# The first products of a hybrid decoder's feed-forward and spatial gate by tokens, 256 or 512 columns wide

## The chip, the core and the metric

The kernel runs on one core of a Trainium2 chip: TensorE (matmuls), VectorE, ScalarE, GpSimd, SyncE (which here only issues transfers) and 16 DMA engines. The metric is the time of one execution on the device in microseconds; the kernel before took 1311.81 us (median of three runs, 1311.23 to 1313.46). In the rows and the code the engines are PE, DVE, ACT, POOL and SP.

## The reference

Two layers, each of three sub-layers with a LayerNorm behind them, on x of 256 tokens by 1024 features in float32:

```python
x = LN(ALPHA*x + 0.5*swiglu(x, ffn_w1[l,0], ffn_w3[l,0], ffn_w2[l,0]))   # D_FF = 2816
y, v_raw = hybrid_mixer(x, w_in[l], gate_b[l], p_branch[l], w_out[l], ...)
x = LN(ALPHA*x + y)
x = LN(ALPHA*x + 0.5*swiglu(x, ffn_w1[l,1], ffn_w3[l,1], ffn_w2[l,1]))

swiglu(x, w1, w3, w2) = (silu(x @ w1) * (x @ w3)) @ w2
hybrid_mixer: z = x @ w_in, cut in r k v w a g | zu zv | lx ly | three gates
  o_rwkv = rwkv7(z[r..g])            # state recurrence, 8 heads of 64
  o_gmlp = gelu(zu) * (tril(ws) @ LN(gelu(zv)) + sb)      # spatial gate, 512 wide
  o_lru  = gelu(ly) * scan(conv(lx))                      # 512 wide
  merged = sum(sigmoid(gate_i) * (o_i @ p_branch[i]));  y = merged @ w_out
```

## The kernel before

**Products.** float32 products are made of two parts of each operand: hi is the value rounded to TensorE's fp32r, lo the rest. `mm3` makes each product of a k block (128 of the 1024 inputs) as three matmuls into one accumulator: hi·hi (L214), hi·lo (L215) and lo·hi (L216). x is held transposed as `xT`, hi and lo, 128 features by 256 tokens for each of eight k. There are two forms of product with x. By features (`feature_wide`, the rows w L328 and L330), a weight block is the stationary side and xT the moving one, 512 columns for hi and lo together. By tokens (`token_major`), xT's 128 tokens of a token tile `tt` (two of them) are the stationary side and the weights the moving one: there the output has tokens on its partitions. Before, a block by tokens is 256 columns wide, so that it takes 8 k × 3 = 24 matmuls a token tile.

**What goes by tokens.** In each of the four FFNs block 0 of w1 and of w3 (the rows w1t, w3t), in each mixer the spatial gate's zv (blocks 9 and 10) and zu (blocks 7 and 8), each as two blocks of 256 columns beside each other in one PSUM bank. All other blocks of the FFN (`up(j)`, j from 1 to 10) go by features. `gate` makes silu(h1)·h3 of block 0, `gtrans` transposes it on TensorE to feature-major (gtr), and `split` cuts that in hi and lo (L219, L220). `down(j)` multiplies g by w2 into four accumulators (the rows dn), 2 tt × 2 halves × 2 k × 3 = 24 matmuls of 512 columns a block.

**Weights.** The class `Weights` holds one queue of pieces in the order of use. A piece is 512 KB; SyncE issues its DMA, ScalarE casts it to hi (whi L104), VectorE subtracts for lo (wlo L106; GpSimd does it for the first block of the second FFN of a layer, POOLW). `use(key)` asks for the next piece, and keeps 4 pieces converted ahead of the one in use; with the three or five loads ahead of that, this is what spreads the transfers and conversions over the program.

**The seams.** Each sub-layer ends in a LayerNorm per token tile and in transposes of its result to the next xT (`x_transposes`, the rows tr, two quarters of four transposes for each token tile). `behind(flush, products, cuts)` places a list of products around the two quarters of token tile 1: all but the last cuts[0] before the first quarter, cuts[0] − cuts[1] between, and cuts[1] after the second. FLUSH gives the cuts in groups of three matmuls, (3, 2): the products of token tile 0 that need only its own half of xT fill the time until the transposes of token tile 1 can run. At the start of the program there is nothing to flush: x comes transposed from memory, and `warm` fills in transposes of the identity (L1407). `FHOLD` is 3: the last three blocks of down products are held back to the end of the FFN.

**The mixer.** Its sub-tasks are interleaved by a table (TUNE) and by priorities; a scheduler that simulates the engines then fixes the order of each engine's instructions, which each engine runs strictly in that order. Part of it is one inverse per layer, for the rwkv recurrence. TensorE makes scores sc (L856), transposes bk and ar·v (bkt L866, avt L872); ScalarE copies them; VectorE masks sc, reduces and scales (vs L878, sv L879), and makes X from sc by transposes (L896) and UT from X (L899, L900). GpSimd then runs 30 short steps, X L918 and UT L919 by turns. VectorE makes X L931, Rd L934 and Tt L935 of the result, and TensorE takes that up with y L941, then z, and a second y L959. In the meantime TensorE works off products of the other branches: lx, zu, gate, sg (the spatial mix), ogt (transposes of the spatial gate's result, L1167), lg (the LRU's small products) and ly.

## Time and profile before

| | us |
|---|---|
| median of three runs (lowest to highest) | 1311.81 (1311.23 to 1313.46) |
| the profiled execution, its own time | 1312.26 |
| its span | 1310.5 |
| TensorE busy (9520 matmuls) | 1285.9 (98%) |
| its weight loads, which overlap the matmuls | 1160.5 (89%) |
| VectorE busy | 939.9 (72%) |
| ScalarE busy | 652.6 (50%) |
| GpSimd busy | 84.1 (6%) |
| DMA, mean over the span | 176 GB/s |

The profile is one execution. Its page gives each engine's busy time, the chain of work that ended last, and the costliest groups of instructions; the trace behind it gives every instruction with its start. Matmuls are pipelined, so the duration of one (0.28 us for 256 columns, 0.39 us for 512) is longer than the distance from its start to the next start. The time of a row of them is therefore read from starts. A wait in a row is the engine's idle time before the instruction, with the instruction on another engine that released it. The granted clock is the share of TensorE's 2.4 GHz that the chip let it have.

### The profile page before, as it was taken

Reading aid. Unit: us, or ns where it says so; the run is one execution under the profiler, and the core shown is the slowest. Engines: PE = TensorE matmul, PEld = TensorE weight load, DVE = VectorE, ACT = ScalarE, POOL = GpSimd, SP = SyncE. Lnnn points to the kernel's source line nnn. Section 1 sums busy time; section 2 is a strip of 40 time slices with the busy share of each in tenths; the row PEclk is TensorE's granted clock in tenths of the full one; section 3 lists DMA queues with packets and bytes.
Section 4 is the critical chain, followed back from the end, with each engine's and each line's share of the span. In section 5 each row is a group of like instructions: output and inputs, shape, how many; then the busy total and the mean of one; then the engine's idle time right before and its main releaser. Section 6 shows DMA issues by size and latency. Waiting matters only on the chain.

```text
span 1310.5 us, 23332 instructions
## 1 busy us (share of the span) xinstructions
PE 1285.9 (98%) x9520; PEld 1160.5 (89%) x9520; DVE 939.9 (72%) x1311; ACT 652.6 (50%) x881; POOL 84.1 (6%) x147
## 2 busy tenths in 40 slices
PE   9999999998999999999999999999989999999997
PEld 8888889997999988888898888999979998888886
DVE  6877666787576678666678766667876667787664
ACT  5654426655845545444255544275557544554440
POOL 1000000003000110000000000001030002100000
PEclk9999999999999999999999999999989999999999
DMA  7885524533345658655259664254332466586630
GB/s 264 296 334 192 176 81 130 177 119 125 98 130 177 209 175 311 220 188 171 93 204 355 210 189 140 66 186 129 130 98 99 129 213 206 177 307 214 189 110 33
DMA packets 66843, 230.87 MB, mean 176 GB/s; under 512 B 8208, under 2 KB 8208, under 8 KB 66736
## 3 DMA queue, kind: packets, MB, share of 16 engines
q1 hardware_dynamic: 66096, 227.29, 51.9%
q0 software_dynamic: 640, 2.10, 0.5%
q8 instruction: 75, 1.23, 0.4%
q14 instruction: 32, 0.26, 0.1%
HBM read 228.30 MB, written 1.05 MB: 175 GB/s over the span
## 4 chain that ended last, share of the span: by engine, by line
PE 92%; DVE 4%; POOL 2%; ACT 1%; issue 1%; DVEq 0%; ACTq 0%; POOLq 0%
PE w L328 22%; PE w L330 11%; PE dn L216 6%; PE dn L215 6%; PE dn L214 6%; PE gate L215 3%; PE gate L216 3%; PE gate L214 3%; PE zr L216 2%; PE zr L215 2%; PE zr L214 2%; PE pb L214 2%; PE pb L216 2%; PE pb L215 2%; DVE wlo L106 1%
## 5 line engine op out<-in xcount | busy, mean ns | idle before, releaser
L106 DVE TENSOR_TENSOR wlo<-raw,whi 128x1024 fp32r<-128x1024 f32 (+1 forms) x314 | 379.0, 1211 | 167.7 <-ACT whi L104 97.0
L104 ACT CAST whi<-raw 128x1024 fp32r<-128x1024 f32 (+1 forms) x322 | 327.8, 1034 | 297.3 <-issue 65.6
L328 PE MATMUL w<-xT,whi 128*128 128x512 f32 x1280 | 320.8, 392 | 0.0
L328 PEld LDWEIGHTS w<-xT,whi 128*128 128x128 f32 x1280 | 232.2, 189 | 43.9
L330 PEld LDWEIGHTS w<-xT,wlo 128*128 128x128 f32 x1280 | 174.6, 190 | 12.5
L330 PE MATMUL w<-xT,wlo 128*128 128x256 f32 x1280 | 178.4, 282 | 0.0
L216 PE MATMUL dn<-w,g 128*128 128x512 f32 x352 | 137.5, 390 | 1.5 <-DVE g L220 1.5
L215 PE MATMUL dn<-w,g 128*128 128x512 f32 x352 | 137.2, 390 | 0.0
L214 PE MATMUL dn<-w,g 128*128 128x512 f32 x352 | 137.2, 390 | 0.0
L106 DVE TENSOR_TENSOR w<-raw,w 128x1024 fp32r<-128x1024 f32 x88 | 105.1, 1221 | 37.0 <-ACT w L104 36.9
L401 DVE TENSOR_REDUCE h<-w 128x256 f32<-128x512 f32 x160 | 109.7, 686 | 12.6 <-PE w L330 11.8
L104 ACT CAST w<-raw 128x1024 fp32r<-128x1024 f32 x88 | 89.4, 1048 | 47.5 <-DMA raw<-in_ffn_w_dram 26.0
L214 PE MATMUL gate<-xT,whi 128*128 128x256 f32 x384 | 109.8, 286 | 0.5 <-DVE xc L1187 0.5
L216 PE MATMUL gate<-xT,wlo 128*128 128x256 f32 x384 | 109.7, 286 | 0.0
L215 PE MATMUL gate<-xT,whi 128*128 128x256 f32 x384 | 109.4, 285 | 0.0
L216 PEld LDWEIGHTS dn<-w,g 128*128 128x128 f32 x352 | 66.1, 188 | 15.6 <-DVE g L220 1.9
L214 PEld LDWEIGHTS dn<-w,g 128*128 128x128 f32 x352 | 66.2, 188 | 12.4
L215 PEld LDWEIGHTS dn<-w,g 128*128 128x128 f32 x352 | 66.1, 188 | 12.4
L214 PEld LDWEIGHTS gate<-xT,whi 128*128 128x128 f32 x384 | 73.5, 191 | 1.7 <-issue 1.5
L216 PEld LDWEIGHTS gate<-xT,wlo 128*128 128x128 f32 x384 | 73.5, 191 | 0.6 <-issue 0.2
L215 PEld LDWEIGHTS gate<-xT,whi 128*128 128x128 f32 x384 | 73.5, 191 | 0.5 <-issue 0.2
L219 ACT CAST g<-gf 128x512 fp32r<-128x512 f32 (+1 forms) x44 | 25.6, 581 | 95.0 <-DVE gf L384 95.0
(335 smaller groups left out, 2247.4 us busy)
## 6 DMA issues: line engine op xcount, KB each, us to landing
raw<-in_ffn_w_dram SPq DMA_DIRECT2D x263, 512.0 KB, 4.4
raw<-in_w_in_dram SPq DMA_DIRECT2D x108, 512.0 KB, 3.9
raw<-in_p_branch_dram SPq DMA_DIRECT2D x24, 512.0 KB, 3.5
raw<-in_w_out_dram SPq DMA_DIRECT2D x16, 512.0 KB, 4.2
ln_g<-in_ln_g_dram SPq DMA_DIRECT2D x8, 256.0 KB, 6.1
ln_b<-in_ln_b_dram SPq DMA_DIRECT2D x8, 256.0 KB, 6.5
bd<-in_bd_dram SPq DMA_DIRECT2D x6, 256.0 KB, 6.2
xt<-in_xt_dram SPq DMA_DIRECT2D x4, 256.0 KB, 4.9
```

The source lines that it names most:

```text
L104: self.last_act = self.nc.scalar.copy(hi[:, s:s + w], t[:, s:s + w]).ins
L106: eng.tensor_tensor(lo[:, s:s + w], t[:, s:s + w], hi[:, s:s + w], ALU.subtract)
L214: mm(out, a[0], b[0], start=start, stop=False)
L215: mm(out, a[0], b[1], start=False, stop=False)
L216: self.last_mm = mm(out, a[1], b[0], start=False, stop=stop).ins
L219: self.split_ins = (self.nc.scalar.copy(hi, src).ins, self.nc.vector.tensor_tensor(lo, src, hi, ALU.subtract).ins)
L328: mm(out, parts[0][k], self.xT2[:, :, k, :], start=k == 0, stop=False)
L330: mm(out[:, 0, :], parts[1][k], self.xT[0][:, k, :], start=False, stop=k == 7)
L401: nc.vector.tensor_reduce(t[:, m, :], b.rearrange("p a s -> p s a"), mybir.AxisListType.X, ALU.add)
```

## The change

Block 0 of w1 and of w3 are laid beside each other in memory as one block of 512 columns, w13, and so are zv's two blocks and zu's two. They come as four pieces of [128, 2, 512], each with two k for all 512 columns, in place of 2 × 2 pieces of [128, 4, 256] with four k for 256 columns; number and bytes of the pieces stay as they were. A product by tokens of them is now one matmul of 512 columns where there were two of 256: 48 in place of 96 for each FFN, zv and zu. The FFN takes one PSUM bank per token tile (w13t) in place of two.

`behind` now gets single matmuls, with FLUSH (5, 3): 19 of 512 columns stand before the first quarter of transposes, 2 between, 3 after. Before it was 39 of 256 columns, 3 and 6. In the first FFN of the program, w13's products go k pair by k pair over both token tiles, the filler after the first six; and the first down products of that FFN are used and queued one block later (after up(3), before after up(2)).

```diff
@@ -40,13 +40,13 @@
 FHOLD = 3
 
 
-POOLW = ("w1", "w3")
+POOLW = True
 
 
 HPX = 200
 
 
-FLUSH = (3, 2)
+FLUSH = (5, 3)
 FTAIL = (2, 2)
 
 
@@ -304,11 +304,17 @@
             for f in products[n - cuts[1]:]:
                 f()
 
-    def token_major(self, out, ws, tt, c0, ks=range(8)):
+    def token_major(self, out, ws, tt, ks=range(8)):
 
         for k in ks:
-            self.mm3(out[:, c0:c0 + 256], [t[:, k, tt * P:(tt + 1) * P] for t in self.xT],
-                     [t[:, k % 4, :] for t in ws[k // 4]], k == 0, k == 7)
+            self.mm3(out, [t[:, k, tt * P:(tt + 1) * P] for t in self.xT], [t[:, k % 2, :] for t in ws[k // 2]], k == 0, k == 7)
+
+    def token_products(self, out, ws, tt):
+
+        def product(k, i, j):
+            self.last_mm = self.nc.tensor.matmul(out, self.xT[i][:, k, tt * P:(tt + 1) * P], ws[k // 2][j][:, k % 2, :],
+                                                 start=k + i + j == 0, stop=k == 7 and i == 1).ins
+        return [lambda a=(k, i, j): product(*a) for k in range(8) for i, j in ((0, 0), (0, 1), (1, 0))]
 
     def feature_major(self, out, ws):
 
@@ -333,11 +339,18 @@
         for q in range(2):
             self.W.add(key + (q,), w[c0 // 256, q], pool=pool)
 
+    def queue_wide(self, key, w, pool=False):
+
+        for q in range(4):
+            self.W.add(key + (q,), w[q], pool=pool)
+
+    def use_wide(self, *key):
+        return [self.W.use(key + (q,)) for q in range(4)]
+
     def use_block(self, *key):
         return [self.W.use(key + (q,)) for q in range(2)]
 
 
-    NTM = 1
     HOLD = FHOLD
 
     def queue_ffn(self, l, f):
@@ -349,14 +362,13 @@
-        for w, nm in ((w1, 'w1'), (w3, 'w3')):
-            for j in range(self.NTM):
-                self.queue_block((l, f, nm, j), w, j * 256, pool=f == 1 and nm in POOLW)
+
+        self.queue_wide((l, f, 'w13'), A['w13'][l, f], f == 1 and POOLW)
         d = 0
-        for j in range(self.NTM, NFF):
+        for j in range(1, NFF):
             self.queue_block((l, f, 'w1', j), w1, j * 256)
             self.queue_block((l, f, 'w3', j), w3, j * 256)
-            if j > self.NTM and d < NFF - self.HOLD:
+            if j > 1 + (l + f == 0) and d < NFF - self.HOLD:
                 down(d)
                 d += 1
         while d < NFF:
@@ -366,7 +378,7 @@
     def ffn(self, l, f, x, flush, out=None, between=None):
 
 
-        nc, W, NTM, HOLD = self.nc, self.W, self.NTM, self.HOLD
+        nc, W, HOLD = self.nc, self.W, self.HOLD
         with ExitStack() as ctx:
             tp = ctx.enter_context(self.tc.tile_pool(name=self.n("ffn"), bufs=2))
             xT = self.xT
@@ -419,60 +431,45 @@
             def use_down(j):
                 return [W.use((l, f, 'w2', j, k)) for k in range(2)]
 
-            first = [(nm, [self.use_block(l, f, nm, j) for j in range(NTM)]) for nm in ('w1', 'w3')]
-            gfs, hs = [], {}
+            first = self.use_wide(l, f, 'w13')
+            hs = [self.bank(self.mm, [P, 512], "w13t") for tt in range(2)]
             if flush is None:
 
-                steps = {'w1': ((0, 0, 2), (0, 2, 4), (1, 0, 4), (0, 4, 8), (1, 4, 8)), 'w3': ((0, 0, 8), (1, 0, 8))}
                 last = None
-                for nm, blocks in first:
+                for k in range(0, 8, 2):
                     for tt in range(2):
-                        hs[tt, nm] = self.bank(self.mm, [P, NTM * 256], nm + "t")
-                    for n, (tt, k0, k1) in enumerate(steps[nm]):
                         with ExitStack() as order:
                             if last is not None:
                                 order.enter_context(self.tc.issue_after(last))
-                            self.token_major(hs[tt, nm], blocks[0], tt, 0, range(k0, k1))
+                            self.token_major(hs[tt], first, tt, range(k, k + 2))
                         last = self.last_mm
-                        if nm == 'w1' and n == 0:
+                        if k + tt == 0:
                             with self.tc.issue_after(last):
                                 last = self.warm(WARM[1])
-            for tt in range(2):
-                ps = []
-                for nm, blocks in first:
-                    if flush is None:
-                        ps.append(hs[tt, nm])
-                        continue
-                    b = self.bank(self.mm, [P, NTM * 256], nm + "t")
-                    ps.append(b)
-                    for j in range(NTM):
-                        if tt == 0 and (nm, j) == ('w3', NTM - 1):
-                            self.behind(flush, [lambda k=k: self.token_major(b, blocks[j], tt, j * 256, [k]) for k in range(8)], FLUSH)
-                        else:
-                            self.token_major(b, blocks[j], tt, j * 256)
-                gfs.append(gate(*ps))
-            for j in range(NTM):
-                gtile(j)
+            else:
+                self.behind(flush, self.token_products(hs[0], first, 0), FLUSH)
+                self.token_major(hs[1], first, 1)
+            gfs = [gate(h[:, 0:256], h[:, 256:512]) for h in hs]
+            gtile(0)
 
             def gtrans(tt):
-                ps = self.bank(self.acc, [P, 2 * NTM, P], "gtr")
-                for i in range(2 * NTM):
+                ps = self.bank(self.acc, [P, 2, P], "gtr")
+                for i in range(2):
                     nc.tensor.transpose(ps[:, i, :], gfs[tt][:, i * P:(i + 1) * P], self.ident)
-                for j in range(NTM):
-                    self.split(*[t[:, :, tt * P:(tt + 1) * P] for t in g[j]], ps[:, 2 * j:2 * j + 2, :])
+                self.split(*[t[:, :, tt * P:(tt + 1) * P] for t in g[0]], ps)
 
             d = 0
-            for j in range(NTM, NFF):
+            for j in range(1, NFF):
                 up(j)
...
-                if j == NTM:
+                if j == 1:
                     gtrans(0)
                     gtrans(1)
-                if j > NTM and d < NFF - HOLD:
+                if j > 1 + (l + f == 0) and d < NFF - HOLD:
                     ws = use_down(d)
                     down(d, ws, 0)
                     down(d, ws, 1)
@@ -590,12 +587,12 @@
         def p(b, j):
             T.W.add((l, 'p', b, j), pb[b, j])
 
-        z(9, 10)
+        T.queue_wide((l, 'zv'), A['w_tok'][l, 1])
         for what, *i in beside(l):
             if what == "z":
                 z(ZBLOCKS[i[0]])
             elif what == "zu" and i[0] == 0:
-                z(7, 8)
+                T.queue_wide((l, 'zu'), A['w_tok'][l, 0])
             elif what == "lx":
                 z(11 + i[0])
             elif what == "ly":
@@ -1106,25 +1103,17 @@
         nc.scalar.activation(q, q, AF.Tanh)
         nc.vector.scalar_tensor_tensor(out, q, 1.0, ps, ALU.add, ALU.mult)
 
-    def token_block(self, blocks, tt, what):
-
-        ps = self.mm([P, 512], what)
-        for i, ws in enumerate(blocks):
-            self.T.token_major(ps, ws, tt, i * 256)
-            yield ps
-
     def zv_first(self):
-        T, nc = self.T, self.nc
-        blocks = [T.use_block(self.l, 'z', b) for b in (9, 10)]
+        T = self.T
+        ws = T.use_wide(self.l, 'zv')
         self.gv = []
         for tt in range(2):
             g = self.mt([P, 512], "gv")
             ps = self.mm([P, 512], "zv")
-            T.token_major(ps, blocks[0], tt, 0)
             if tt == 0:
-                T.behind(self.flush, [lambda k=k: T.token_major(ps, blocks[1], tt, 256, [k]) for k in range(8)], FLUSH)
+                T.behind(self.flush, T.token_products(ps, ws, tt), FLUSH)
             else:
-                T.token_major(ps, blocks[1], tt, 256)
+                T.token_major(ps, ws, tt)
             self.gelu2(ps, g)
             self.gv.append(g)
 
@@ -1133,11 +1122,13 @@
         v = nc.vector
         og = [self.mp.tile([P, 2, S], F32R, tag="m", name=T.n("ogT")) for i in range(4)]
         self.og = [[og[0], og[1]], [og[2], og[3]]]
-        blocks = [T.use_block(self.l, 'z', b) for b in (7, 8)]
+        ws = T.use_wide(self.l, 'zu')
         us = []
         for tt in range(2):
             u = self.mt([P, 512], "u")
-            for pu in self.token_block(blocks, tt, "zu"):
+            pu = self.mm([P, 512], "zu")
+            for k in (0, 4):
+                T.token_major(pu, ws, tt, range(k, k + 4))
                 yield self.ZUS
             self.gelu2(pu, u)
             us.append(u)
@@ -1482,8 +1473,16 @@
     r = {n: a[n] for n in big}
 
     r['xt'] = a['x'].reshape(2, P, 2, 4, P).transpose(0, 2, 4, 3, 1)
+    def by_tokens(w):
+        w = w.reshape(w.shape[:-2] + (4, 2, P, 512))
+        i = w.ndim - 4
+        return w.transpose(tuple(range(i)) + (i, i + 2, i + 1, i + 3))
+
     for n in ('ffn_w1', 'ffn_w3', 'w_in'):
         r[n] = pieces(a[n])
+
+    r['w13'] = by_tokens(np.concatenate([a['ffn_w1'][..., 0:256], a['ffn_w3'][..., 0:256]], -1))
+    r['w_tok'] = np.stack([by_tokens(a['w_in'][..., c * 256:(c + 2) * 256]) for c in (7, 9)], 1)
     r['p_branch'] = pieces(a['p_branch'])[:, :, :, 0]
     r.update(vecs=vecs, wsm=wsm, bd=bd)
     return {n: np.ascontiguousarray(t) for n, t in r.items()}
```

The order in three places, each as the instructions stand on their engine.

TensorE in layer 1, where the 19 products of zu that stand behind the last sc end and the transposes of the inverse begin; zu is the spatial gate's product, bkt and avt are the inverse's transposes. Before, then after:

```order
L214 MATMUL zu_10152<-whi_9945,xT_8750 128x256
L866 MATMUL bkt_9879<-ident,bk_9670 128x128 x4
L215 MATMUL zu_10152<-wlo_9946,xT_8750 128x256
L216 MATMUL zu_10152<-whi_9945,xT_8750 128x256
L872 MATMUL avt_9886<-ident,arv_9669 128x128 x4
```

```order
L214 MATMUL zu_9850<-whi_9731,xT_8496 128x512
L863 MATMUL bkt_9577<-ident,bk_9368 128x128 x4
L869 MATMUL avt_9584<-ident,arv_9367 128x128 x2
L863 MATMUL bkt_9593<-ident,bk_9368 128x128 x4
L869 MATMUL avt_9600<-ident,arv_9367 128x128 x2
L869 MATMUL avt_9584<-ident,arv_9367 128x128
```

The products of zu are as many and twice as wide; the first avt, whose four transposes came in one piece behind one bkt, is now parted around the second bkt.

VectorE in layer 1, from the work beside GpSimd's steps to the transposes that y takes up (wlo is a weight piece's subtraction, X L931 or L928 reads GpSimd's last step, u belongs to the spatial gate, xc to the LRU). Before, then after:

```order
L106 TENSOR_TENSOR wlo_10142<-raw_10127,whi_10141 128x1024
L1187 SCALAR_TENSOR_TENSOR xc_10023<-lx_10024,vecs_7883,xc_10023 128x253
L931 TENSOR_SCALAR X_9915<-UT_9920,bsel 128x16x16 x2
L106 TENSOR_TENSOR wlo_10148<-raw_10133,whi_10147 128x1024
L934 STREAM_TRANSPOSE Rd_10283<-X_9915 128x16x2x16
L1160 SCALAR_TENSOR_TENSOR u_10151<-sg_10302,vecs_7883,u_10151 128x128 x4
L106 TENSOR_TENSOR wlo_10392<-raw_10139,whi_10391 128x1024
L935 STREAM_TRANSPOSE Tt_10284<-Rd_10283 128x512
```

```order
L106 TENSOR_TENSOR wlo_9840<-raw_9825,whi_9839 128x1024
L1178 SCALAR_TENSOR_TENSOR xc_9721<-lx_9722,vecs_7629,xc_9721 128x254
L106 TENSOR_TENSOR wlo_9846<-raw_9831,whi_9845 128x1024
L1178 SCALAR_TENSOR_TENSOR xc_9721<-lx_9722,vecs_7629,xc_9721 128x253
L928 TENSOR_SCALAR X_9613<-UT_9618,bsel 128x16x16 x2
L1151 SCALAR_TENSOR_TENSOR u_9849<-sg_9952,vecs_7629,u_9849 128x128 x4
L106 TENSOR_TENSOR wlo_10042<-raw_9837,whi_10041 128x1024
L931 STREAM_TRANSPOSE Rd_9933<-X_9613 128x16x2x16
L932 STREAM_TRANSPOSE Tt_9934<-Rd_9933 128x512
```

One wlo has moved from behind X L931 to ahead of it, among the work beside GpSimd.

TensorE in layer 0, ahead of the second group of scores. Before (34 products of lx stand there, then 14 more of lx and 9 of gate behind the scores), then after (all 48 of lx and 12 of gate ahead, 17 of gate behind):

```order
L216 MATMUL lx_3131<-xT_1897,wlo_2780 128x256
L214 MATMUL lx_3131<-xT_1897,whi_2779 128x256
L215 MATMUL lx_3131<-xT_1897,whi_2779 128x256
L216 MATMUL lx_3131<-xT_1897,wlo_2780 128x256
L214 MATMUL lx_3131<-xT_1897,whi_2779 128x256
L856 MATMUL sc_3050<-arv_2902,bk_2903 128x128
```

```order
L214 MATMUL gate_3093<-xT_1839,whi_2795 128x256
L215 MATMUL gate_3093<-xT_1839,whi_2795 128x256
L216 MATMUL gate_3093<-xT_1839,wlo_2796 128x256
L853 MATMUL sc_2896<-arv_2772,bk_2773 128x128
L853 MATMUL sc_2897<-arv_2772,bk_2773 128x128
```

The scores have moved behind 26 more products of 256 columns. In both layers, four of the ogt transposes now stand ahead of y.

## Rows read from the trace of the kernel before

**Rows 1.** The page, parts 1 and 4: busy us (share) and count; chain's shares.
```profile
PE 1285.9 (98%) x9520; PEld 1160.5 (89%) x9520; DVE 939.9 (72%) x1311; ACT 652.6 (50%) x881; POOL 84.1 (6%) x147
...
PE 92%; DVE 4%; POOL 2%; ACT 1%; issue 1%; DVEq 0%; ACTq 0%; POOLq 0%
```

**Rows 2.** TensorE's waits: line, releaser, us in total, times, longest us.
```profile
PE y L941 <- DVE Tt L935: 9.1, 2, 5.3
...
PE dn L216 <- DVE g L220: 1.5, 1, 1.5
```

**Rows 3.** Timeline of TensorE: start us, duration us, engine, line, operation, xcount.
```profile
182.64 0.39 PE L214 MATMUL dn<-w,g 128*128 128x512 f32 x1
...
191.26 0.39 PE L216 MATMUL dn<-w,g 128*128 128x512 f32 x1
...
193.75 0.28 PE L214 MATMUL zv<-whi,xT 128*128 128x256 f32 x1
...
198.30 0.28 PE L216 MATMUL zv<-whi,xT 128*128 128x256 f32 x1
```

**Rows 4.** Chain in order of time, first FFN: start us, us on the chain, what.
```profile
19.11 1.84 PE w L328 x8
```

**Rows 5.** Timeline of TensorE at the program's start.
```profile
5.04 0.58 PE L214 MATMUL w1t<-whi,xT 128*128 128x256 f32 x1
...
6.73 1.47 PE L1407 MATMUL warm<-ident 128*128 128x128 f32 x9
```

**Rows 6.** Timeline of TensorE at the first down products; brackets: idle before, releaser.
```profile
41.95 0.40 PE L215 MATMUL dn<-w,g 128*128 128x512 f32 x1
43.83 0.50 PE L216 MATMUL dn<-w,g 128*128 128x512 f32 x1 [1.48 <-DVE g L220]
```

**Rows 7.** Chain in order of time, layer 1's inverse.
```profile
937.95 1.99 PE sc L856 x32
...
943.08 0.45 PE avt L872 x4
943.55 0.59 ACT at L875
944.17 0.70 DVE vs L878
...
947.48 0.97 DVE X L896
...
955.45 0.31 POOL X L918
...
955.83 1.19 POOL UT L919
...
968.84 1.13 DVE wlo L106
```

**Rows 8.** Timeline of VectorE beside GpSimd's steps, layer 1.
```profile
955.54 1.28 DVE L106 TENSOR_TENSOR wlo<-raw,whi 128x1024 fp32r<-128x1024 f32 x1
...
957.66 1.21 DVE L106 TENSOR_TENSOR wlo<-raw,whi 128x1024 fp32r<-128x1024 f32 x1
```

**Rows 9.** Timeline of VectorE, layer 0's inverse.
```profile
291.89 2.36 DVE L106 TENSOR_TENSOR wlo<-raw,whi 128x1024 fp32r<-128x1024 f32 x2
294.16 0.68 DVE L878 TENSOR_REDUCE vs<-avt 64x8 f32<-64x512 f32 x1
...
320.17 0.46 DVE L1187 SCALAR_TENSOR_TENSOR xc<-lx,vecs,xc 128x255 f32<-128x255 f32 x1
320.55 0.70 DVE L935 STREAM_TRANSPOSE Tt<-Rd 128x512 f32<-128x512 f32 x1
```

**Rows 10.** Stretches: us, busy of PE, PEld, DVE, ACT, POOL; granted clock; DMA share; GB/s.
```profile
322.00:327.00 5.00, 4.80 (x117) 4.41 (x109) 3.60 (x9) 3.59 (x10) 0.00 (x0) 0.72 0.59 193
...
970.00:975.00 5.00, 4.26 (x136) 3.96 (x137) 4.19 (x9) 3.80 (x7) 0.00 (x0) 0.50 0.36 110
975.00:980.00 5.00, 5.00 (x144) 4.00 (x144) 3.51 (x7) 3.72 (x11) 0.00 (x0) 0.82 0.69 209
```

## The prediction, made before the changed kernel ran

> **What bounds the kernel now.** I read the page first: TensorE is busy for 98% of the span and carries 92% of the chain that ended last [rows 1]. So a saved microsecond of TensorE counts almost anywhere, except where TensorE itself waits. Next I read its waits: the longest by far are the two at y L941, 9.1 us together (5.3 in layer 1, so 3.8 in layer 0), then 1.5 us at the first down product [rows 2]. The reader should see that this splits the program in two kinds of stretch. In the one, time is the number of products times their spacing. In the other, around the inverse in each layer, time is set by a chain sc → avt → X → GpSimd → Tt → y; TensorE's work that lies beside this chain costs nothing, and whatever delays the chain's start costs in full. The span is 1310.5 us, the profiled run took 1312.26 us, so 1.8 us lie around it; the median of 1311.81 is 0.45 us lower. I sum against 1312.26.
>
> **Part 1, half as many products of twice the width.** 39 starts of 256-column products lie between 193.75 and 198.30 us, 38 gaps of 0.1197 us; 39 of 512 columns between 182.64 and 191.26, 38 gaps of 0.2268 [rows 3]. Two narrow ones cost 0.2394, a wide one saves 0.0126. The other wide row is up's, eight in 1.84 us, 0.230 each [rows 4], a saving of 0.0094. I take 0.2268, since its products have the changed ones' form (two different weights a k, no doubled moving tile).
> Three later FFNs, 96 narrow to 48 wide each: 3 × 48 × 0.0126 = −1.8 us (−1.35 by the other row). For zv in two layers it is 2 × 48 × 0.0126 = −1.2 us (−0.9). For zu it is −0.6 a layer, which is beside the chain or ahead of it; it is counted in parts 4 and 5. The first FFN would save −0.6 too, but the program's first products are slower: six narrow ones take from 5.04 to 6.73 us, 0.28 each, before nine fillers [rows 5]. Six wide ones in their place move twice the columns at that pace, at most 1.69 us more; six narrow ones fewer remain afterwards at 0.12 (−0.7), so up to +1.0 net. With the −0.6, the bounds are −0.6 and +0.4; I take 0. The transfers don't change this: four pieces of 512 KB before and after, in the same place of SyncE's queue, each enough for 2.9 us of narrow products (24) before and 2.7 us of wide ones (12) now.
>
> A rule weighed here. The spacings of [rows 3] are 119.7 and 226.8 ns. The Trainium skill, "TensorE: Matmul & The Clock Gate", section "Back-to-back issue gap", gives an isolated spacing of N/2.4 + 2.5 ns, 109.2 and 215.8, of which a pair would save only 2.5 ns: 0.6 us over the 240 pairs of the later FFNs and zv. The trace disagrees by 10 and 11 ns, and the sum goes by the trace.
>
> **Part 2, down products a block later in the first FFN.** The third down product should start at 41.95 + 0.23 = 42.18 and starts at 43.83, having waited for VectorE's g L220 [rows 6]: 1.65 us lost. Another block of up now stands between (four times eight wide products and eight narrow, 4 × (1.84 + 0.96) = 11.2 us by [rows 3, 4]), so that wait goes: −1.65. The w2 pieces are queued a block later too, so SyncE's queue serves them no later against their use. Bounds −1.65 and 0, the latter if the first up block, which now ends without a down product behind it, waits as long for its own weights.
>
> **Part 3, the transposes of the next xT.** Behind the LayerNorm, 39 narrow products covered the wait ahead of the first transposes; 19 wide ones do now: 39 × 0.1197 = 4.67 against 19 × 0.2268 = 4.31, 0.36 less cover. No transpose that waits for the LayerNorm stands in the list of TensorE's waits, so how much slack there is doesn't show. At five boundaries: 0 to 1.8; I take +0.2, as the absent wait speaks for slack.
>
> **Part 4, layer 1's inverse.** This is the largest term. Before, 19 narrow zu products stand between the scores (937.95 to 939.94) and the transposes bkt, behind which avt follows at 943.08, and ACT's copy of it releases vs L878, behind which X L896 stands on VectorE at 947.48 [rows 7]. The same 19 products are now wide: 18 × 0.1071 = +1.9 us, and the transposes are interleaved so that the first avt ends after both bkt, +0.5. avt ends at 945.98 instead of 943.53: X +2.5 us, since VectorE runs in order. On GpSimd a step takes 0.31 us, but 1.19 where a wlo of VectorE (955.54, 957.66) runs beside it [rows 7, 8]. Three wlo, not two, now stand in that stretch: +0.88. One wlo fewer stands between the stretch and Tt (968.84, 1.13 us on the chain [rows 7]): −1.13. So y is 2.25 us later; four ogt transposes, which came behind it, now stand ahead in its wait: −0.44, by four avt transposes of the same shape [rows 7]. Since zu's −0.6 lies in the wait, the layer pays **+1.8**. Bounds: if VectorE catches up and X starts as before, −0.7 (−1.13 + 0.88 − 0.44); if three more GpSimd steps rather than one are stretched, +3.6.
>
> **Part 5, layer 0's inverse.** Before the scores there are now all 48 lx products and 12 of gate where 34 lx stood: 26 × 0.1197 = +3.1, and zu's −0.6 is ahead of them: scores +2.5 us. From there on 17 products stand before bkt where 23 did, −0.7, so avt is 1.8 later and vs, which came behind two wlo at 294.16 and now waits for avt alone, 1.4 later; but one wlo (1.13) now stands between vs and X: X +2.5 [rows 9]. A fourth wlo beside GpSimd +0.88, one fewer behind it −1.13, one more xc step (0.38 from its start to the next [rows 9]) +0.4: y +2.65; ogt −0.44. **+2.2**. Bounds as above: −0.3 where X doesn't move, +4.
>
> **Part 6, the clock.** Behind the wait of layer 1 the granted clock is 0.50 of 970 to 975 us and 0.82 of the next five [rows 10]: after an idle stretch TensorE runs at 1.2 GHz for a while, then at 2.4. Longer waits put other products in that stretch, 128×256 ones instead of the 32×32 ones of y. I take +0.5; bounds 0 and +2.8 (below).
>
> Sum: −1.8 − 1.2 + 0 − 1.65 + 0.2 + 1.8 + 2.2 + 0.5 = **+0.05**: 1312.3 for a profiled run, **1311.9** for the median. What the products save is paid back where the wider zu and the moved lx hold up the inverses.
>
> **Rivals.** *The inverses are not later* (faster). VectorE has idle time behind GpSimd, and if the copies and masks, not avt, set X, parts 4 and 5 give −0.7 and −0.3. Then −3.0 − 1.65 + 0.2 − 1.0 = −5.45, with no longer wait and so nothing for the clock: 1306.4. With one layer only it is some 1309, at the edge of what can be told; it is counted here. For it: X is behind other VectorE work in both traces. Against: in layer 1 the chain runs through avt and ACT without a gap [rows 7].
> *The clock stays low longer* (slower). A stretch that is at 0.50 for 5 us longer than now loses half of it, 2.5 us, plus what y and ogt lose in the second layer, 0.3: +2.8, 1314.7. It decides from the point where TensorE's wait at y passes from 5.3 to about 7.5 us. For it: 970 to 975 shows it at a wait of 5.3 [rows 10]. Against: layer 0 waited 3.8 and shows 0.72 right behind it [rows 10], so the loss grows slowly with the wait.
> *No saving in the products* (slower): a wide one takes what two narrow ones take, 0.2394. The −3.0 is gone, and so is zu's −0.6 ahead of layer 0's scores: +3.6, 1315.5. Against it stand both rows of wide products [rows 3, 4]; for it, that no product of this form is 512 wide with xT as the stationary side before. Beside it stands the page named above: by its spacing 0.6 us of the 3.0 would remain, 1314.9.
>
> **How the numbers follow.** Forecast 0.50, faster rival 0.28, clock 0.15, no saving 0.07. The forecast's own range, with one of parts 3 to 6 at a bound (one X not later: −2.5; two more GpSimd steps stretched, or the clock: +1.8 to +2.3), is 1309.4 to 1314.2, all within 0.2% (2.6 us, about what a measurement of this kernel tells from no change). For 8 in 10 the range reaches to the faster rival's time, which leaves about one in ten below it, and past the slower ones': 1306.4 to 1315.0. Faster by over 0.2%: 0.28; within: 0.50; slower: 0.22.
>
> **What would show it.** Wide products at 0.227 in w13t, zv and zu; no wait at the first down product; in layer 1 the first X of VectorE 2.5 us later behind the last sc than the 7.55 us of before, and the wait at y L941 (now L938) near 8 us in both layers. If the waits at y stay at 5.3 and 3.8, the forecast is too high by 4 us. If w13t's spacing is 0.24, it is too low by 3. If a new wait appears at a transpose of the next xT, part 3 was too small.

## The result, and the profile after

The changed kernel takes **1324.99 us** (median of four runs, 1322.63 to 1328.02), the kernel before 1312.63 beside it (1311.23 to 1313.54). The ratio is 1.0092, with a 95% interval of 1.0075 to 1.0109: slower by 0.9%, outside the predicted range. The profiled run took 1324.55 us, its span is 1322.8.

The page of the kernel after, parts 1 and 4, against [rows 1]: busy us, share and count, then the chain's shares.

```profile
PE 1290.7 (98%) x9136; PEld 1144.7 (87%) x9136; DVE 938.8 (71%) x1307; ACT 651.8 (49%) x877; POOL 86.4 (7%) x147
...
PE 90%; DVE 5%; POOL 2%; ACT 2%; issue 1%; DMA 1%; SPq 0%; DVEq 0%; ACTq 0%; POOLq 0%
```

There are 384 matmuls fewer, and yet TensorE is busy for 4.8 us more. Its idle time grew by 7.5 us: 1322.8 − 1290.7 = 32.1 where 1310.5 − 1285.9 = 24.6 stood. So more than one thing happened. To place it, I cut both spans at the same points: a mixer begins at the first transposes (tr) that bring its xT, and ends at the first product of the next FFN. The loss to the clock is the sum of (1 − granted clock) × 2.5 us over stretches of 2.5 us.

| us | FFN 0,0 | mixer 0 | FFN 0,1 | FFN 1,0 | mixer 1 | FFN 1,1 | mixer 0: idle; loss to the clock | mixer 1: the same |
|---|---|---|---|---|---|---|---|---|
| before | 191.49 | 275.77 | 184.05 | 185.42 | 280.33 | 193.44 | 6.45; 3.43 | 6.19; 3.42 |
| after | 190.08 | 289.56 | 183.74 | 184.87 | 281.39 | 193.16 | 14.18; 8.53 | 6.84; 5.15 |
| difference | −1.41 | **+13.79** | −0.31 | −0.55 | +1.06 | −0.28 | +7.7; +5.1 | +0.7; +1.7 |

The whole loss lies in layer 0's mixer. Not all of the clock's column is a cost: of the 8.53 us, 2.1 lie between 321.1 and 325.3 us, where TensorE is idle anyway. While it is busy, mixer 0 loses 3.3 us before and 6.4 after (+3.1), mixer 1 3.0 and 4.7 (+1.7). Its stretch in the two kernels (us, busy of PE, PEld, DVE, ACT, POOL, granted clock, DMA share, GB/s), before:

```profile
191.50:467.30 275.80, 269.36 (x2724) 256.71 (x2723) 202.51 (x310) 158.26 (x240) 34.88 (x51) 0.99 0.44 142
```

and after:

```profile
190.00:479.50 289.50, 275.33 (x2628) 256.57 (x2626) 203.42 (x310) 158.42 (x240) 35.46 (x51) 0.97 0.42 135
```

VectorE, ScalarE and GpSimd have the work they had. TensorE has 96 matmuls fewer, a lower mean clock and more idle time. What it waits for now (line, releaser, us in total, times, longest), against [rows 2]:

```profile
PE lg L1184 <- DVE xc L1178: 6.7, 1, 6.7
...
PE gate L214 <- DVE xc L1178: 3.9, 1, 3.9
...
PE y L956 <- DVE Tt L947: 2.9, 1, 2.9
...
PE lx L214 <- DVE u L1104: 2.3, 1, 2.3
```

The wait at the first y has left layer 0. Two waits on VectorE that were not there before stand in its place: lx for u, and lg for xc. The gate's wait of 3.9 is in layer 1. TensorE's timeline of the kernel after in mixer 0 (start, duration, what; in brackets the idle time before and its releaser):

```profile
272.73 0.22 PE L655 MATMUL rs<-identr,sw 128*128 128x128 f32 x1
...
282.86 0.39 PE L214 MATMUL lx<-xT,whi 128*128 128x256 f32 x1 [2.28 <-DVE u L1104]
...
291.73 2.16 PE L853 MATMUL sc<-arv,bk 64*128 64x128 f32 x32
...
325.31 2.04 PE L1184 MATMUL lg<-xc,bd 128*128 128x256 f32 x4 [6.73 <-DVE xc L1178]
...
328.13 1.93 PE L938 MATMUL y<-Tt,UB 32*32 32x32 f32 x128
```

The same of the kernel before:

```profile
271.57 0.22 PE L658 MATMUL rs<-identr,sw 128*128 128x128 f32 x1
...
287.02 2.16 PE L856 MATMUL sc<-arv,bk 64*128 64x128 f32 x32
...
321.39 1.93 PE L941 MATMUL y<-Tt,UB 32*32 32x32 f32 x128 [3.79 <-DVE Tt L935]
```

From the mixer's start (191.49 before, 190.08 after) rs is 2.6 us later, these scores 6.1 and y 8.2. VectorE's timeline of the kernel after names what TensorE waited for:

```profile
282.11 0.69 DVE L1104 SCALAR_TENSOR_TENSOR u<-gq,zu 128x512 f32<-128x512 f32 x1
...
322.93 0.61 DVE L928 TENSOR_SCALAR X<-UT,bsel 128x256 f32<-128x256 f32 x2 [3.96 <-POOL UT L916]
...
324.75 0.41 DVE L1178 SCALAR_TENSOR_TENSOR xc<-lx,vecs,xc 128x253 f32<-128x253 f32 x1
325.09 0.68 DVE L932 STREAM_TRANSPOSE Tt<-Rd 128x512 f32<-128x512 f32 x1
```

Neither wait is for data. lx takes the PSUM bank that held zu of token tile 0, and the bank is free once VectorE has read it for u. lg's second accumulator takes the bank of lx block 1, and that is free once VectorE has read lx for its last convolution step xc. That step stands in VectorE's queue behind X of the inverse, which waits for GpSimd. So lg, and the ogt transposes and y behind it on TensorE, wait for the inverse by way of a bank. That lx and lg wait for banks is read from the code and the releasers here; for lg it is tested below (lg_acc). In the kernel before, lg stood ahead of y as well, but its bank was one of a gate, and it waited for ScalarE's reading of that gate:

```profile
316.47 1.13 PE L1193 MATMUL lg<-xc,bd 128*128 128x256 f32 x4 [0.74 <-ACT gate L1250]
```

Idle time and clock are not all of it. Behind the inverse, the recurrence runs as 208 small products (s, up and o) between larger ones. Before, eight of one kind stand in a row; after, they alternate in twos for part of the way. Before, then after:

```profile
372.82 0.45 PE L1002 MATMUL s<-state,w2t 64*64 64x64 f32 x8
373.11 0.40 PE L1006 MATMUL o<-arv,state 64*64 64x64 f32 x8
```

```profile
375.21 0.33 PE L999 MATMUL s<-state,w2t 64*64 64x64 f32 x2
375.47 0.33 PE L1015 MATMUL up<-sv,bkt 128*64 128x64 f32 x2
```

Eight of s take 0.29 us there, two take 0.26 here. The order changes 28 times directly from a product of the form 64*64 (the field behind the names) to one of 128*64 or back, where it never did before; from the start of the product ahead of such a change to the next start it is 0.15 us, between two products of the same form 0.03 to 0.05. From start to next start, without the idle time, the 208 products take 8.4 us before and 13.2 after: +4.7.

Idle time +7.7, the clock while TensorE is busy +3.1, the recurrence +4.7, and some −1.2 for the wide zv and zu (2 × 48 × 0.0126) make 14.3 of the 13.8 that were measured. The half microsecond between them stays open.

### The profile page after: what moved, and what is told of

Same layout as the page of the kernel before. It is cut to its first block, busy times and chain, and to the rows that moved or that the text cites. A ratio compares the mean times of both kernels' runs of the same rounds, so it can differ in the third digit from the quotient of the medians.

```text
span 1322.8 us, 22543 instructions
## 1 busy us (share of the span) xinstructions
PE 1290.7 (98%) x9136; PEld 1144.7 (87%) x9136; DVE 938.8 (71%) x1307; ACT 651.8 (49%) x877; POOL 86.4 (7%) x147
## 4 chain that ended last, share of the span: by engine, by line
PE 90%; DVE 5%; POOL 2%; ACT 2%; issue 1%; DMA 1%; SPq 0%; DVEq 0%; ACTq 0%; POOLq 0%
PE w L334 22%; PE w L336 12%; PE dn L216 6%; PE dn L215 6%; PE dn L214 6%; PE gate L216 3%; PE gate L214 3%; PE gate L215 3%; PE zr L216 2%; PE zr L215 2%; PE zr L214 2%; PE pb L214 2%; PE pb L216 2%; PE pb L215 2%; DVE wlo L106 1%; PE wo L216 1%
## 5 line engine op out<-in xcount | busy, mean ns | idle before, releaser
L336 PEld LDWEIGHTS w<-xT,wlo 128*128 128x128 f32 x1280 | 174.6, 190 | 12.5
L214 PE MATMUL gate<-xT,whi 128*128 128x256 f32 x384 | 111.8, 291 | 3.9 <-DVE xc L1178 3.9
L215 PE MATMUL gate<-xT,whi 128*128 128x256 f32 x384 | 110.6, 288 | 0.0
L214 PEld LDWEIGHTS dn<-w,g 128*128 128x128 f32 x352 | 66.2, 188 | 12.5
```

The lines of the kernel that those rows point to most:

```text
L214: mm(out, a[0], b[0], start=start, stop=False)
L215: mm(out, a[0], b[1], start=False, stop=False)
L336: mm(out[:, 0, :], parts[1][k], self.xT[0][:, k, :], start=False, stop=k == 7)
```

## The experiments

All edits are against the changed kernel. Ratios are to the kernel before in runs on the same chip, with 95% intervals.

**zu of 256 columns again (zu_narrow).** Old pieces and old products for zu, the rest as after; layer 0's order is then that of before.

```diff
-                T.queue_wide((l, 'zu'), A['w_tok'][l, 0])
+                z(7, 8)
-            for k in (0, 4):
-                T.token_major(pu, ws, tt, range(k, k + 4))
+            for i in range(2):
+                T.token_narrow(pu, blocks[i], tt, i * 256)   # the old token_major
```

> The changed kernel with only zu as before: 256 columns in the old pieces; the FFNs and zv stay 512 wide. Theory A (the whole loss is what wide zu does to the order around the inverses): layer 0's mixer comes back from 289.56 to some 275 us (275.77 of before less 0.6 for zv), layer 1's from 281.39 to some 279.7; with the 2.55 us that the four FFNs gained, 1312.6 - 2.55 - 1.2 = 1308.9. Rival B (the loss comes from the new pieces or the earlier start of the mixer, whatever zu does): layer 0's mixer stays above 285 us and the time above 1320.

Measured: 1311.9 us, ratio 0.9987 (0.9972 to 1.0002). Mixer 0 takes 279.01 us with 6.39 idle, mixer 1 279.16 with 6.42. Without the wide zu the loss is gone, and so are both new waits; the recurrence takes 8.4 us as before. The time is 3 us above the expected 1308.9: mixer 0 lost 8.5 us to the clock in this profile, 5.1 more than in the profile of before.

**The same in layer 0 alone (zu0_narrow).** The edit above where `self.l == 0`.

> zu as before in layer 0 alone, wide in layer 1. Theory A with layer 1's part as predicted (y 2.25 us later, the clock): layer 1's mixer stays at 281.4, layer 0's comes back to 275; 1308.9 + 1.7 = 1310.6. Rival: zu's price in layer 1 was paid by something that came over from layer 0, then this is 1308.9 as with both narrow.

Measured: 1318.63 us, 1.0052 (1.0035 to 1.007), 8 us above what was expected. Mixer 0 is as in zu_narrow (279.36 us, idle 6.98), which places the cost in layer 0's zu. But mixer 1, whose order is that of after, took 285.95 us instead of 281.39: its loss to the clock was 8.50 (after: 5.15) and its idle time 9.38 (6.84), 2.1 of it behind no releaser that the profile names:

```profile
PE z L954 <- issue: 2.1, 1, 2.1
```

**lg moved behind other work in the table (tune_lg1).**

```diff
-    ... lg,0 ot,1 lg,1 g,2,2 ls ...
+    ... lg,0 ot,1 g,2,2 lg,1 ls ...
```

> The changed kernel, and in layer 0 the LRU's second small products (lg) one gate block later in the table, so that they stand behind y on TensorE. If y is held up by lg (which waited 6.7 us for VectorE's xc and ended 2.4 us after Tt): y at 325.7 instead of 328.1 and 1322.5. If the inverse was late by rs behind 24 wide zu and what follows y has slack anyway: within 1 us of 1325.

Measured: 1320.24 us, 1.0062 (1.0045 to 1.008). A miss: the edit moved the wrong half. The waiting product belongs to lg,0 (its second accumulator), and its wait is unchanged in the timeline of this run:

```profile
326.27 2.04 PE L1184 MATMUL lg<-xc,bd 128*128 128x256 f32 x4 [6.73 <-DVE xc L1178]
...
329.09 1.93 PE L938 MATMUL y<-Tt,UB 32*32 32x32 f32 x128
```

Still the time is 4.8 us below that of the kernel after. The table moved much else in mixer 0 (284.24 us): the recurrence's products stand together by form again, with one change in place of 28, and take 8.6 us in place of 13.2. That is about the gain, with the wait of lg left as it was.

**The first down products as early as before (nodelay).**

```diff
-            if j > 1 + (l + f == 0) and d < NFF - self.HOLD:
+            if j > 1 and d < NFF - self.HOLD:
```

> The changed kernel with the first FFN's down products used and queued as early as before. If the wait at the first down product was what the delay saved: the wait of 1.5 us is back and the time is 1325.0 + 1.65 = 1326.6. If the 1.41 us of the first FFN came from the wide products or the new start: 1325.0, and no wait at dn.

Measured: 1327.49 us, 1.0114 (1.0094 to 1.0135). TensorE at the third down product, where [rows 6] showed a wait of 1.48:

```profile
44.45 0.39 PE L216 MATMUL dn<-w,g 128*128 128x512 f32 x1
```

No wait, although the delay is undone. But this doesn't show that the delay is needless, because the program started more slowly in this run: TensorE waited for a weight piece, and the clock was low behind it, from 8.5 to 11.9 us. VectorE's g, for which the third down product had waited in the kernel before, comes no more than 0.5 us earlier than there (42.82, before 43.36):

```profile
7.75 0.50 PE L214 MATMUL w13t<-whi,xT 128*128 128x512 f32 x1 [1.40 <-ACT whi L104]
...
42.82 0.75 DVE L220 TENSOR_TENSOR g<-gtr,g 128x256 fp32r<-128x256 f32 x2
```

The first of up's products starts at 21.22 us here and at 19.34 in the kernel after. With that start, the third down product would have come at 44.45 − 1.88 = 42.57, ahead of g: an estimate, by which some 0.7 us of wait would be left. So it stays open how much of the wait the delay removes and how much the wide first block. The time is not explained by either expectation: the first FFN takes 191.97 us (190.08 after) by its slow start, and mixer 0 291.1 (289.56).

**The wide zu tied behind the chain (chain_wide).** zu's products are issued behind rs and avt in both layers.

```diff
+                T.chain_mm = nc.tensor.matmul(...).ins      # rs; the same for avt
+                with T.tc.issue_after(T.chain_mm):
                     T.token_major(pu, ws, tt, range(k, k + 4))
```

> The changed kernel, with zu's wide products tied behind the transposes rs and avt of the inverse's chain on TensorE: in layer 0 rs stands behind 12 wide zu after avt in place of 24, in layer 1 no product stands between the last sc and bkt where 19 wide ones did (4.3 us). Theory C (the chain to the inverse is late because wide products stand ahead of rs and avt): in layer 1 the wait at y falls by some 4 us and the mixer from 281.4 to 277.4; in layer 0 rs is 2.7 us earlier, y at least 5, the mixer from 289.6 to some 282; 1325 - 11.6 = 1313.4. Rival D (the waits come from VectorE's own queue, with the weight pieces and the LRU's steps): y moves by less than 1 us in both layers, 1323 to 1325.

Measured: 1310.87 us, 0.9992 (0.9982 to 1.0001), which is 14 us less than after with the same products. Mixer 0 takes 272.46 us with 5.59 idle, 3.3 us less than in the profile of before, of which 1.7 are less loss to the clock. TensorE in this kernel:

```profile
268.59 0.22 PE L655 MATMUL rs<-identr,sw 128*128 128x128 f32 x1
...
318.94 1.93 PE L938 MATMUL y<-Tt,UB 32*32 32x32 f32 x128 [3.19 <-DVE Tt L932]
```

and VectorE, whose u comes 8.7 us earlier than in the kernel after, counted from the mixer's start:

```profile
274.76 0.69 DVE L1104 SCALAR_TENSOR_TENSOR u<-gq,zu 128x512 f32<-128x512 f32 x1
```

From the mixer's start at 191.43, rs is 2.9 us earlier than before and y 2.4. lx and lg don't wait; y waits for Tt again, and the recurrence takes 7.7 us, with no change of form inside. It is thus not the width of zu that costs, but what order and banks came with it. Mixer 0 is 10 us shorter than theory C had it, which knew neither the banks nor the recurrence. In mixer 1 the tie does nothing (282.32 us): the first avt is 3.3 us earlier there than after, but X is only 1.4 earlier. On VectorE it stands behind the bonus (943.13 to 943.82), which waits for TensorE's bon, and bon now stands behind 16 of the tied zu.

**The tie with the narrow zu (chain_narrow).** The tie of chain_wide on zu_narrow.

> As with zu of 256 columns (its FFNs and zv 512 wide), and zu tied behind rs and avt. Theory C: layer 1's 19 narrow products (2.3 us) go from ahead of bkt, its mixer from 279.2 to some 277; in layer 0 rs comes some 1 us earlier; 1311.9 - 3 = 1309. Rival D: within 1 us of 1311.9.

Measured: 1312.57 us, 1.0007 (0.9994 to 1.002); mixer 0 278.30, mixer 1 279.99. The tie gains nothing with narrow products, whose layer 0 had no bank wait to lose.

**New pieces, narrow matmuls (zu_pieces).** zu's four pieces as after, its matmuls 256 wide.

```diff
+            for h in (0, 256):
+                for k in range(8):
+                    T.mm3(pu[:, h:h + 256], ..., [t[:, k % 2, h:h + 256] for t in ws[k // 2]], k == 0, k == 7)
```

> The changed kernel with zu's pieces as changed (two k for 512 columns), but its products of 256 columns, first half and then second. rs stands behind as many narrow products as before, the last sc of layer 0 behind all of zu. If the products' width ahead of rs and avt makes the loss: some 1312 to 1315, near the kernel with zu wholly as before (1311.9). If the pieces (other order of k, conversions that come earlier) make it: 1320 or more.

Measured: 1317.88 us, 1.0031 (1.0013 to 1.005). Mixer 0 takes 279.08 us with 10.41 idle. There is no lg wait, but y waits longer, and 1.8 us without a named releaser:

```profile
PE y L938 <- DVE Tt L932: 6.2, 1, 6.2
...
PE y L938 <- issue: 1.8, 1, 1.8
```

The order is a third one, so this run doesn't split width from pieces cleanly. Its time lies between the two that were expected. It shows that without the lg wait, and with the recurrence at 7.8 us, longer waits at y alone can leave 4 us of idle time more than before.

**The FFN alone (ffn_only).** zv and zu as before the change.

> The wide form in the FFNs alone, zv and zu as before. The FFNs' gains as profiled in the changed kernel, -1.41, -0.31, -0.55 and -0.28, give 1312.6 - 2.55 = 1310.1, and 1.2 us more than with zv wide, if zv's products save what their spacing says. If the mixer's start (zv, with the seam's cuts) costs something instead, this is not slower than the kernel with zv wide, 1311.9.

Measured: 1314.04 us, 1.0011 (1.0001 to 1.0022). The FFNs take 189.28, 182.61, 184.88 and 193.18. Mixer 0, whose products and order are those of before, took 283.76 us in the profiled run, 8 more than in the profile of before: 5.1 are loss to the clock, 2.9 idle time, of which 1.93 at one transpose of the next xT. I had not expected this, and it led to the last run.

**lg in the other PSUM pool (lg_acc).**

```diff
-        pg = [self.mm([P, 2, S], "lg") for _ in range(2)]
+        pg = [(self.mm if self.l else self.acc)([P, 2, S], "lg") for _ in range(2)]
```

> The changed kernel, and in layer 0 the LRU's small products lg write accumulators of the other PSUM pool; the order up to them is the changed kernel's. There the second pair took the bank of lx's second block, which VectorE's last convolution step frees only behind the inverse. Theory E (the 6.7 us wait of lg is for that bank): it falls under 1 us, 23 gate products come ahead of y, y starts at Tt (325.8 in place of 328.1), and with less lost to the clock the time is 1325 - 5 = 1320. Rival (lg waits for its own data, xc): the wait stays above 5 us and the time within 1.5 us of 1325.

Measured: 1320.16 us, 1.0048 (1.0034 to 1.0062); mixer 0 281.48. lg hardly waits now, but a gate product, which takes the bank instead, does:

```profile
319.46 1.10 PE L1184 MATMUL lg<-xc,bd 128*128 128x256 f32 x4 [0.17 <-ACT xc L1176]
...
327.30 0.55 PE L214 MATMUL gate<-xT,whi 128*128 128x256 f32 x1 [6.30 <-DVE xc L1178]
```

The wait is the bank's: whoever comes next in it waits for the last xc, and a gate product reads no xc. So theory E is right on the bank. Its time came out too, but by luck. The 23 gate products that now come ahead of y all stand behind the wait, and y is later than in the kernel after, 140.6 us from the mixer's start in place of 138.1:

```profile
332.48 1.40 PE L938 MATMUL y<-Tt,UB 32*32 32x32 f32 x128
```

Of the 8.1 us that mixer 0 gained, 2.5 are idle time and 5.4 the recurrence, whose products stand together by form here (7.8 us in place of 13.2).

**Filler in lg's wait (fill_lg).** 52 transposes of the identity, whose result nobody uses, between lg's two accumulators.

```diff
+                    with T.tc.issue_after(last):
+                        for q in range(52):
+                            last = nc.tensor.transpose(wb[:, q % 4, :], T.ident, T.ident).ins
```

> The changed kernel, and in layer 0 52 transposes of the identity (0.11 us each) between the first and the second pair of lg, work that nobody uses; y comes behind 47 of them, ahead of the second pair. If the wait also costs by the clock: no stretch at 0.50 follows at 325 to 333, some 2.5 us less, and with y 2.3 us earlier 1325 - 4.8 = 1320. If the clock falls whatever TensorE does there: 1322.7 with y's part alone.

Measured: 1327.93 us, 1.0109 (1.009 to 1.0127). Mixer 0 is 1.35 us shorter than after, its loss to the clock 5.12 instead of 8.53. Filler and y in the timeline:

```profile
318.53 5.29 PE L1188 MATMUL fill<-ident 128*128 128x128 f32 x47
...
326.02 1.28 PE L938 MATMUL y<-Tt,UB 32*32 32x32 f32 x128 [2.20 <-DVE Tt L932]
...
329.74 1.12 PE L1188 MATMUL fill<-ident 128*128 128x128 f32 x4 [2.18 <-issue]
```

The granted clock is full through the filler and falls only later, at 327.7 us. In this kernel from 317.5 to 335 us:

```profile
317.50:327.50 10.00, 7.71 (x180) 7.21 (x180) 5.15 (x10) 2.35 (x8) 4.49 (x14) 1.00 0.34 107
327.50:335.00 7.50, 5.32 (x19) 4.48 (x19) 2.15 (x4) 4.38 (x11) 0.00 (x0) 0.54 0.01 2
```

and in the kernel after, where it falls at 321.1 us, in the wait:

```profile
317.50:327.50 10.00, 3.27 (x10) 2.38 (x11) 5.04 (x10) 2.37 (x8) 4.38 (x14) 0.68 0.32 105
```

But TensorE isn't busy all the way here: it waits 2.20 us at y and 2.18 in the filler, and the low stretch follows these. So in this profile the clock didn't fall whatever TensorE did; how much of the clock's loss the wait causes stays open. The recurrence has 24 of its changes of form and takes 12.5 us, and mixer 1 took 5.2 us more in another order, so the total says nothing on this.

**What the runs point to (best_b).** The wide FFN and zv; layer 0's zu wide and tied, layer 1's zu narrow and untied; cuts (3, 2) at the seams.

> Wide in the FFNs, zv and layer 0's zu; layer 0's zu tied behind rs and avt; layer 1's zu as before; the cuts of the seams 3 and 2 in place of 5 and 3. If layer 0's mixer is 272.5 as in the kernel with both ties, and layer 1's 279.2 as with zu narrow: 1310.9 - 3.1 = 1307.8 and faster than before by 0.3%. If the run-to-run state of the clock takes it back as it did with zu narrow: 1311, the same as before.

Measured: 1309.82 us (12 runs) against 1313.8 (20 runs), ratio **0.9973** (0.996 to 0.9986): 0.3% faster than the kernel before. Its mixer 0:

```profile
189.50:461.90 272.40, 266.97 (x2628) 250.32 (x2627) 201.63 (x310) 157.37 (x240) 35.84 (x51) 0.99 0.46 144
```

It is 3.4 us shorter than before's, of which 1.7 are less loss to the clock, with as many matmuls (2628) as took 289.5 in the kernel after. The cuts and the tie were changed together, so what each gives isn't told apart.

**The kernel before, profiled again (before_again).** No edit.

> The kernel before, profiled a second time. Its first profile lost 3.4 us to the clock in each mixer, at a mean granted clock of 0.994; kernels with the same order in layer 0's mixer lost 8.5 there, with a stretch at 0.50 around the first scores. If that stretch comes and goes from run to run with the same program, a run at 0.989 to 0.991 shows it here too and takes some 3 us more (1313.5 to 1316); if it belongs to the changed kernels, this profile has none at 262 to 270 us whatever the time.

Measured: 1314.39 us, mean clock 0.991 where the first profile had 0.994. The program and its order are the same; around layer 0's first scores the granted clock is not. That stretch in the first profile of before:

```profile
262.50:270.00 7.50, 7.50 (x57) 6.97 (x57) 4.88 (x11) 1.69 (x3) 1.65 (x1) 1.00 0.15 57
```

in the second:

```profile
262.50:270.00 7.50, 7.50 (x38) 6.91 (x38) 2.86 (x8) 0.98 (x2) 1.64 (x1) 0.63 0.10 40
```

TensorE is busy throughout in both, and does 38 matmuls in place of 57. Mixer 0 was 279.38 us this time instead of 275.77. So of two single profiles, 3.6 us of a mixer's difference can be chance. The profile of the kernel after has no such stretch there: its granted clock is 1.00 from 262.5 to 270 us, and its three low stretches in mixer 0 begin at 283.5, 321.1 and 345.0, at or just behind its waits of lx, lg and the second y. How long such a stretch behind a wait lasts also varies: behind the same wait at y it is 3.4 us in the first profile of before and 6.8 in the second. The idle time hardly varies: 7.19 in the second profile, 6.45 in the first, 14.18 after. Nor does the recurrence: 8.5 and 8.4, 13.2 after.

## Why the prediction was wrong

**The step that failed is part 5, layer 0's inverse**: +2.2 was summed, less 0.6 for zv, and mixer 0 lost 13.79. Part 5 priced every instruction that moved by its length and took all else to run as before. It put nothing for the PSUM banks, which the new order hands out anew (the waits of lx and lg, and y behind lg), and nothing for the recurrence behind the inverse, whose small products the scheduler mixed (+4.7). Step by step:

- *Scores +2.5 by products.* They are 6.1 later. rs alone is 2.6 later: up to it stand all 48 wide zu, where 66 narrow ones stood, 48 × 0.2268 − 66 × 0.1197 = +3.0, less 0.6 for zv (24 wide in chain_wide, where rs is early). VectorE's u stands behind the work that waits for rs, and the bank for which lx waits stands behind u. The rest is that wait of 2.28 and a stretch of low clock behind it, about 1.7. So the products are about 6.1 − 2.3 − 1.7 = +2.1, beside 2.5 − 0.6 = 1.9 as summed. Right as far as it went: the products were counted, and the bank behind one of them was not.
- *Scores to Tt: +0.2 and no more, y −0.44 by ogt.* Tt is at 135.0 us from the mixer's start instead of 129.1, +5.9 and so 0.2 less than the scores: this step was small, as summed in its parts. But y is +8.2. ogt was priced as free work in y's wait. lg, which stood ahead of y before and after, holds that wait itself now: it is released at 325.16, 6.6 us after TensorE came to it, and lg and ogt then take till 328.13, 2.4 us behind the end of Tt. The work ahead of y was no filler any more but stood in its way.
- *Idle time.* It is +7.7: lx 2.28, lg 6.73 and 1.04 against 0.74, the second y 2.88 instead of 1.08, `up` 0.75, less the 3.79 of the first y that are gone, together 8.1; smaller waits that are gone make the rest.
- *The recurrence.* It is +4.7, for which the prediction has no term. The kernels with its mixed order (after, nodelay, fill_lg) take 12.5 to 13.2 us there, all others 7.7 to 8.6.

What was missing is the bank and the order further on. The order of instructions shows who comes before whom, not that two of them share a buffer. lg_acc shows the bank: the product that takes it in lg's place waits as lg did. chain_wide shows that all of it goes with another order of the same products, and tune_lg1 that most of the recurrence's part can go while the wait of lg stays.

**Part 4, layer 1's inverse**, was right in its steps. The chain of the kernel after in layer 1, against [rows 7]:

```profile
949.00 1.99 PE sc L853 x32
...
955.96 0.22 PE avt L869 x2
...
960.96 0.99 DVE X L893
...
968.96 1.20 POOL X L915
...
970.62 1.17 POOL X L915
...
972.26 1.18 POOL X L915
```

X starts 960.96 − 950.99 = 9.97 us behind the last sc, before 7.54: +2.4, predicted +2.5. Three GpSimd steps are stretched instead of two, as predicted. Mixer 1 lost 1.06 us where 1.8 − 0.6 = 1.2 were summed. That the two agree is in part luck: idle time grew by only 0.7, and the clock lost 1.7 more, where part 6 had +0.5 for both layers. The sign for it was wrong: y's wait did not grow to 8 but fell to 1.4, and 3.9 stand at a gate ahead of it, again behind xc; that this is a bank too is not tested in layer 1. Chain_wide shows that avt is not all that sets X: an avt 3.3 us earlier gave 1.4.

**Part 1** was right in kind. The first and the last of 18 matmuls of a wide zu:

```profile
951.25 0.39 PE L215 MATMUL zu<-wlo,xT 128*128 128x512 f32 x1
...
955.13 0.40 PE L214 MATMUL zu<-whi,xT 128*128 128x512 f32 x1
```

That is 3.88 / 17 = 0.228 us each against the 0.2268 taken, so the rival without a saving falls. The spacing of 0.2158 that "TensorE: Matmul & The Clock Gate" of the Trainium skill, section "Back-to-back issue gap", gives for an isolated matmul isn't met by this row either. The three later FFNs gained 0.31, 0.55 and 0.28, together 1.14 where 1.8 less part 3's 0.2 were summed.

**Part 3** was a little too small, as its sign said: transposes that wait for the LayerNorm cost 0.2 us each at two places, 0.4 in all beside the 0.2 taken.

```profile
PE tr L290 <- DVE x L259: 0.4, 2, 0.2
```

**Part 2** was right in size: −1.41 for the first FFN beside −1.65, and the wait at the down products is gone. Whether the delay alone did it stays open (nodelay). The program's start fits part 1's estimate: six wide products take 2.82 us, six narrow ones 1.69 [rows 5], so 1.1 more where at most 1.69 was allowed.

```profile
4.95 0.80 PE L214 MATMUL w13t<-whi,xT 128*128 128x512 f32 x1
...
7.77 1.14 PE L1398 MATMUL warm<-ident 128*128 128x128 f32 x9
```

**Part 6, the clock**, was too small: +0.5 with a bound of +2.8, measured +3.1 in mixer 0 and +1.7 in mixer 1 while TensorE was busy. It came not by a longer wait at y, as the rival had it, but at lx, around lg and at the gate; how much of it single profiles owe to chance stays open (before_again). At an equal mean clock of 0.990, runs of the kernel before took 1313.6 to 1316.0 us and the one run of the kernel after 1322.6: most of the loss isn't the clock's.

## What to carry to other kernels

Where a scheduler hands out PSUM banks, a changed order is also a changed assignment of banks: for each product that moves, look who held its bank last and what that reader waits for, above all where the reader stands behind a long chain on an in-order engine. Work that moves ahead of a waiting instruction fills its wait only if it can run by then; if it has a wait of its own, it delays what it was to hide. When fewer, wider products change the order around a latency chain, try them tied behind the chain's own instructions (it helped in layer 0, not in layer 1), and judge the width after that: here the same matmuls cost +0.9% untied and −0.1% (not told from none) tied in both layers. With the tie in layer 0, layer 1's zu narrow and the old cuts it was −0.3%. And look at the order further on: small products of two forms that alternate can cost more than the wait that one was looking at.

## What the runs showed of the hardware

The same program has a stretch at a granted clock of 0.50 (1.2 of 2.4 GHz) in one run and not in another, with TensorE busy all through it (262.5 to 270 us of the kernel before: 1.00 and 0.63). Runs of the kernel before with a mean clock of 0.993 to 0.994 took 1310.1 to 1312.5 us, those with 0.989 to 0.991 1312.7 to 1317.9; a difference of 0.3% between single profiles is nothing unless the idle time or the order shows it too. In the kernel after, the clock falls to 0.50 at 321.1 us, within the wait of lg, and is full again at 331.3, with TensorE busy since 325.3; this costs only while TensorE is busy.

Small products cost by their neighbours: where a 64*64 product and a 128*64 one follow each other directly, 0.15 us lie between their starts, and 0.03 to 0.05 between two of the same form. The 28 such changes in layer 0's recurrence of the kernel after go with 4.7 us.
